# Pads and a new order of the SBUF pools in a two-layer decoder kernel: tiles that TensorE reads brought to multiples of 512 bytes

## The chip, the cores and the metric

The kernel runs on one core of a Trainium2 chip. The metric is device time in microseconds (us) of one launch, which holds the whole computation; weights are re-cut on the host before the launch and come from HBM. The kernel before was run three times: median 2026.53 us, from 2025.38 to 2033.36.

## The reference

Two decoder layers over x of 512 tokens x 1024 channels, in float32:

```python
for l in range(2):
    x = x + 0.5 * rmsnorm(swiglu_1(rmsnorm(x, g0)), g1)
    x = x +       rmsnorm(mixer_l(rmsnorm(x, g2)), g3)
    x = x + 0.5 * rmsnorm(swiglu_2(rmsnorm(x, g4)), g5)
# swiglu(h) = (silu(h @ wg) * (h @ wu)) @ wd, inner width 2816
# mixer_0: a gated depthwise causal convolution of 31 taps with LayerNorm and SiLU over 512 channels,
#          beside sliding-window attention (8 query heads, 2 key heads, ALiBi, sinks); both into one w_out
# mixer_1: "FoX", causal attention of 16 heads with forget gates, then w_out
```

## The kernel before, in words

**Products.** Every large float32 product is done in three passes of type float32r. An operand is split into `hi` and `lo` (`split`, L65: ScalarE makes `hi`, VectorE or GpSimd subtracts), and `mm3` (L69 to L74) adds hi.hi, hi.lo and lo.hi into one PSUM tile, on the lines 72, 73 and 74. Each pass is a load of 128 stationary columns and one product that streams the moving operand, mostly 512 columns of 4 bytes, 2048 bytes of each partition. In the profile's names `mm<-hhi,whi` the moving operand comes first, the stationary one second.

**Order of the work.** A SwiGLU half step (`ffn`, L188) works in eleven groups of two blocks of 128 inner columns. For each group, `gate_up` streams the normed tokens hT (`hhi`, `hlo`, channels on partitions, eight slices of 512 tokens) past four weight units of 1024 columns (`whi`, `wlo`), 24 products a unit, 96 a group; `evac` makes the activations `ahi`, `alo`. `down` of the group before streams the down weights (again `whi`, `wlo`) past `ahi`, `alo`: 48 products a group, four token blocks x two blocks x two halves x three passes. The first group and the last use products of 256 columns (`first_projs`, L102; `gate_up_half`, L260). The even mixer (`even`, L296) projects 14 units, runs the convolution's taps on VectorE, ScalarE and GpSimd while TensorE projects, then the attention, the LayerNorm and the output projection from `cT` (`chi`, `clo`). The odd mixer (`odd`, L552) projects 16 heads between the heads' scores and values. The queues' order is planned by the framework (line 887), which also sets the waits. All loads of weights go through the SP queue into the three `raw` buffers.

**Where tiles lie.** Pools are laid behind one another in each SBUF partition. Those on the left begin at byte 16512, in the order of their opening, and each tile is rounded up to 32 bytes; those on the right end at byte 229344. Within a pool the tiles follow in the order in which they are first asked for. Worked out by these sizes, the remainders of the start addresses modulo 512 are:

| tile | read by TensorE as | before | after the change |
|---|---|---|---|
| hT: `hhi`, `hlo` (pool `keep`) | moving in projections, stationary for the values of FoX | 224 | 0 |
| `whi`, `wlo` of the rings, and of `dring` on the left | stationary in projections, moving in down | 352 | 0 |
| `whi`, `wlo` of `dring` on the right (layer 1, second half step) | the same | 480 | 0 |
| `ahi`, `alo` | stationary in down | 352 | 0 |
| `chi`, `clo` | stationary in the output projection | 480 even, 352 odd | 0 |
| q, k, v of the even mixer | both | 480 | 0 |
| q, k, v tiles and `pT` of FoX | both | 352 | 0 |
| `yv` | moving, plain float32 | 352 | 0 |
| `wk` work tiles | stationary in transposes | 224 | 0 |
| `ident`, `ident16`, `tri` | transposes and masks | 128, 160, 416 | 288, 320, 64 |
| `alibi`, `ones` | masks, sums of the LayerNorm | 480, 160 | 64, 64 |

All slices that the products take step by multiples of 512 bytes, but for the first four FoX value weights, whose rows are 1088 bytes long (`VF = 256 + H`, L589).

**Names and lines that the steps touch.** `junk` (L132) is where ScalarE's squares for the norms go; nothing reads it. `ones` (L800) is read by the LayerNorm's sums (L480, L491, L502). `alibi` (L538) is built on GpSimd at the start of the even mixer and read by its scores (L414). `dring` (L193) is the down weights' pool. `rstd` (L122) is the norm's part on GpSimd.

Of the kernel before, what the change touches and what calls it, by code (L numbers as in the profile page):

```python
"""Two decoder layers (macaron SwiGLU, conv + sliding-window mixer, forgetting-attention mixer).

Every float32 product with large operands runs on the tensor engine in three float32r passes: an
operand is split exactly into hi (12 significant bits) and lo = x - hi (the other 12), and
a.b = hi.hi + hi.lo + lo.hi is accumulated in float32 PSUM.

Layouts: x is token-major, [128 tokens, 1024] for each of the four token blocks. A pre-norm's result
is transposed into channel-major hi/lo tiles [128, k, 512 tokens], which every projection reads.
"""
# [9 lines left out]
F32 = mybir.dt.float32  # L19
# [7 lines left out]
P = 128  # L27
S = 512
# [12 lines left out]
class Kernel:  # L41
    def __init__(self, ctx, tc, a):
        self.ctx, self.tc, self.nc, self.a = ctx, tc, tc.nc, a
        pool = lambda name, bufs, **kw: ctx.enter_context(tc.tile_pool(name=name, bufs=bufs, **kw))
        self.const = pool("const", 1)
        self.keep = pool("keep", 1)
        self.raws = pool("raws", 3)
        self.work = pool("work", 7)
        self.small = pool("small", 4)
        self.mm = pool("mm", 4, space=PSUM)  # L50
        self.acc = pool("acc", 4, space=PSUM)
# [17 lines left out]
    def mm3(self, out, a, b, start, stop):  # L69
        """out (+)= a.T @ b, each operand a (hi, lo) pair."""  # L70
        mm = self.nc.tensor.matmul
        mm(out, a[0], b[0], start=start, stop=False)  # L72
        mm(out, a[0], b[1], start=False, stop=False)  # L73
        mm(out, a[1], b[0], start=False, stop=stop)  # L74
# [6 lines left out]
    def unit(self, src, inner, pool=None, eng=None):  # L81
        """A [128, 1024] piece of a weight, loaded and split; its (hi, lo) as [128, 1024/inner, inner]."""
        pool = pool or self.ring
        raw = self.loaded.pop(0) if self.loaded else self.load(src)
        hi, lo = (pool.tile([P, 1024], F32R, name=n)[:, : raw.shape[-1]] for n in ("whi", "wlo"))
        with ExitStack() as after:
            for ins in self.guard:
                after.enter_context(self.tc.issue_after(ins.ins))
            self.split(hi, lo, raw, eng)
        return [z.rearrange("p (k c) -> p k c", c=inner) for z in (hi, lo)]  # L90

    def proj(self, out, u, toks=slice(0, S), m=P):
        """out[m, toks] = u.T @ h, u a unit of m columns."""
        for k in range(KD):
            self.mm3(out, [z[:, k, :m] for z in u], [z[:, k, toks] for z in self.hT], k == 0, k == KD - 1)
# [6 lines left out]
    def first_projs(self, srcs, pooled=3, pool=None):  # L102
        """Four units at once, the first half of the tokens ahead of the second."""
        units = [self.unit(s, P, pool, self.nc.gpsimd if n < pooled else None) for n, s in enumerate(srcs)]
        out = [self.psum() for _ in units]
        for half in range(2):
            toks = slice(half * 256, half * 256 + 256)
            for n, (o, u) in enumerate(zip(out, units)):
                self.proj(o[:, toks], u, toks)
                if self.begin:  # L110
                    self.begin.pop(0)()
                if n % 2:
                    self.turn()
        self.guard = self.turned
        return out
# [6 lines left out]
    def rstd(self, ss, eps):  # L122
        """(ss[0] + ss[1] + eps) ** -0.5 for a [128, 2] tile."""
        nc = self.nc
        ms = self.small.tile([P, 1], F32, name="ms")
        nc.gpsimd.tensor_scalar(ms, ss[:, 0:1], ss[:, 1:2], eps, ALU.add, ALU.add)
        r = self.small.tile([P, 1], F32, name="rstd")
        nc.gpsimd.tensor_tensor(r, ms, self.mhalf, ALU.pow)  # L128
        return r

    def square_sum(self, out, src, scale):
        junk = self.work.tile([P, 512], BF16, name="junk", bufs=1)  # L132
        self.nc.scalar.activation(junk, src, AF.Square, scale=scale, accum_out=out)  # L133

    def post(self, t, ys, gain, half_step):
        """x[t] += (0.5 or 1) * rmsnorm(y) * gain; ys are y's two halves, the later one last."""
# [13 lines left out]
    def pre(self, t, gain, order=(0, 1), helper=None):  # L150
        """h[t] = rmsnorm(x[t]) * gain, transposed and split into hT."""
# [18 lines left out]
    def turn(self, n=1):  # L170
        """Transposes and splits the pre-norm's oldest n token blocks that still wait for it."""
# [16 lines left out]
    def ffn(self, l, s, norms, nxt, held=None):  # L188
        nc, tc, a = self.nc, self.tc, self.a
        wg, wu, wd = (a[w][l, s] for w in ("ffn_w_gate", "ffn_w_up", "ffn_w_down"))  # L190
        with ExitStack() as ctx:
# [54 lines left out]
            gate_up(0)  # L246
            if held:
                held.close()
# [3 lines left out]
            # the last two groups of the down projection a token block at a time, the last group's gate  # L252
            # and up half the tokens at a time, so that the norms run under the other half's products
# [42 lines left out]
    def even(self, l, i, nxt):  # L296
# [3 lines left out]
        with ExitStack() as ctx:  # L300
# [6 lines left out]
            cw = late.tile([P, NC, CK], F32, name="cw")  # L307
            conv, att = ExitStack(), ExitStack()
# [4 lines left out]

            sink = pc.tile([P, 8], F32, name="sink")
# [5 lines left out]
            # per-channel parameters, channels on partitions  # L320
            cwr = self.wk()
            nc.sync.dma_start(cwr[:CK, :], a["conv_w"][i])
            for n, v in enumerate(("conv_b", "conv_ln_g", "conv_ln_b")):
                nc.sync.dma_start(vec[:, n, :], a[v][i].rearrange("(c p) -> p c", p=P),
# [12 lines left out]
            def glu(c, sg, pu):  # L337
                """u * sigmoid(gate), with the convolution's zeros ahead of it."""
# [10 lines left out]
            # the depthwise causal convolution: the later taps as products on ScalarE summed on GpSimd  # L349
# [19 lines left out]
            # q tile t holds heads t and t + 4, so that each lies on its kv head's partitions  # L369
            q = [pc.tile([P, NC, S], F32R, name=n) for n in ("qhi", "qlo")]  # L370
            k = [pc.tile([P, S], F32R, name=n) for n in ("khi", "klo")]
            v = [pc.tile([P, NT, P], F32R, name=n) for n in ("vhi", "vlo")]
# [25 lines left out]
            # sliding window attention; ALiBi and the window as one additive bias per head  # L398
# [70 lines left out]
            cT = [cat.tile([P, KD, S], F32R, name=n) for n in ("chi", "clo")]  # L469
            for c in range(NC):  # L470
# [6 lines left out]
            # LayerNorm over the conv channels (partitions): sums through the tensor engine  # L477
# [18 lines left out]
            # to all channels: ones.T @ diag(rstd)  # L496
# [11 lines left out]
            # the attention's half of the output projection  # L508
# [29 lines left out]
    def alibi(self, pool):  # L538
        """Per head, minus slope * distance inside the window and NEG outside it; exact in bfloat16."""
# [12 lines left out]
    def odd(self, l, i, nxt):  # L552
# [3 lines left out]
        with ExitStack() as ctx:  # L556
# [8 lines left out]
            # A head's scores in two products of 128 rows: qa.ka = qhi.khi - c (through a selector of the  # L565
            # head's rows of -c) and qc.kc = qhi.klo + qlo.khi
# [20 lines left out]
            # the values of four heads, [keys, head, (hi, lo), 64]; the first four's weights lie beside the gates'  # L587
# [19 lines left out]
            # c = cumsum(log sigmoid(zf + b_f)), heads on partitions;  # L607
            # log sigmoid(z) = min(z, 0) - log(1 + exp(-|z|))
            def gates():
# [10 lines left out]
                # minus c as hi (rows 64..) and lo (rows 96..)  # L620
# [32 lines left out]
            def transposed(pr):  # L653
                """Blocks of key tile kb, queries kb * 128 .. 512, as (hi, lo)."""
# [13 lines left out]
            def values(h, at):  # L668
# [6 lines left out]
                # rows 0..63 hold v's hi part, the others its lo part  # L675
# [12 lines left out]
            def early(t):  # L688
                """The first 12 heads' part of the output projection's later half."""
# [68 lines left out]
    def run(self):  # L758
        nc, a = self.nc, self.a
        self.x = [self.keep.tile([P, D], F32, name=f"x{t}") for t in range(NT)]  # L760
# [13 lines left out]
        # the clock of an idle tensor engine is halved: products that nothing reads, until x is there  # L774
# [23 lines left out]
    def constants(self):  # L798
        nc = self.nc
        self.ones = self.const.tile([P, P], F32, name="ones")  # L800
        nc.gpsimd.memset(self.ones, 1.0 / CC)
        self.ident16 = self.const.tile([P, P], BF16, name="ident16")
        nc.gpsimd.tensor_copy(self.ident16, self.ident)
        # 0 where key <= query, else NEG
# [3 lines left out]
        # pick[p, h] = 1 where p % 32 == h, for partitions 0..47 and 64..111  # L808
# [15 lines left out]
def _laid_out(i):  # L824
    """The arrays as the kernel reads them: each weight cut into [128, 1024] pieces, every piece contiguous."""
    import numpy as np

    def stationary(w):
        """[n, 1024, C] -> [n, C/128, 128 rows, 8 * 128]: column tile, row in its row tile, (row tile, column)."""
# [3 lines left out]
    def moving(w):  # L833
        """[n, 1024, 1024] -> [n, column half, row tile pair, 128 rows, 2 * 512]."""
# [9 lines left out]
    # conv gates and inputs by turns, k, v, then q heads t and t + 4 side by side  # L844
# [46 lines left out]
```

## Time and profile before

| what | value |
|---|---|
| median of three runs, lowest, highest | 2026.53, 2025.38, 2033.36 us |
| span of the profiled execution | 2025.8 us |
| the profiled execution's own time | not listed apart from the span; the span stands 0.7 us under the median |
| TensorE busy | 1951.0 us, 96% |
| VectorE, ScalarE, GpSimd busy | 986.5, 727.6, 285.5 us |
| mean granted TensorE clock | 0.974 |
| moved by DMA | 178.91 MB, 88 GB/s |

The span runs from the first to the last instruction on the core. [...]

### The profile page before, as it was taken

Reading aid. Unit: us, or ns where it says so; the run is one execution under the profiler, and the core shown is the slowest. Engines: PE = TensorE matmul, PEld = TensorE weight load, DVE = VectorE, ACT = ScalarE, POOL = GpSimd, SP = SyncE. Lnnn points to the kernel's source line nnn. Section 1 sums busy time; section 2 is a strip of 40 time slices with the busy share of each in tenths; the row PEclk is TensorE's granted clock in tenths of the full one; section 3 lists DMA queues with packets and bytes.
Section 4 is the critical chain, followed back from the end, with each engine's and each line's share of the span. In section 5 each row is a group of like instructions: output and inputs, shape, how many; then the busy total and the mean of one; then the engine's idle time right before and its main releaser. Section 6 shows DMA issues by size and latency. Waiting matters only on the chain.

```text
span 2025.8 us, 23961 instructions
## 1 busy us (share of the span) xinstructions
PE 1951.0 (96%) x9694; PEld 1630.3 (80%) x9694; DVE 986.5 (49%) x1351; ACT 727.6 (36%) x1230; POOL 285.5 (14%) x280
## 2 busy tenths in 40 slices
PE   8999999994899999999999999999999989999998
PEld 7888888883578888888988888898888888888887
DVE  6333333589866333333553333346666564333333
ACT  5322221363564322221342222226666543222221
POOL 2000000486512000000300000014222220000001
PEclk8999999997699999999999999999999999999999
DMA  6423232122022423232143232303112224232311
GB/s 213 130 83 104 83 104 73 44 63 73 21 74 93 136 84 103 91 99 76 54 160 104 83 104 87 100 23 113 54 42 65 95 81 139 91 103 84 104 53 42
DMA packets 51407, 178.91 MB, mean 88 GB/s; under 512 B 7361, under 2 KB 7361, under 8 KB 51296
## 3 DMA queue, kind: packets, MB, share of 16 engines
q1 hardware_dynamic: 51296, 177.38, 27.1%
q8 instruction: 76, 1.25, 0.3%
q14 instruction: 35, 0.29, 0.0%
HBM read 175.26 MB, written 2.10 MB: 88 GB/s over the span
## 4 chain that ended last, share of the span: by engine, by line
PE 84%; DVE 8%; ACT 3%; POOL 2%; issue 1%; DMA 1%; SPq 0%; POOLq 0%; DVEq 0%; ACTq 0%
PE mm L73 23%; PE mm L72 23%; PE mm L74 23%; PE acc L72 4%; PE acc L73 4%; PE acc L74 4%; DVE yv L356 4%; ACT junk L133 1%; DVE wlo L67 1%; PE mm L663 1%; PE mm L673 1%; PE acc L182 1%; POOL rstd L128 1%; DVE hlo L67 1%; DVE x L148 1%
## 5 line engine op out<-in xcount | busy, mean ns | idle before, releaser
L72 PE MATMUL mm<-hhi,whi 128*128 128x512 f32 (+1 forms) x1952 | 705.6, 364 | 13.6 <-DVE av L340 8.7
L73 PE MATMUL mm<-hlo,whi 128*128 128x512 f32 (+1 forms) x1952 | 707.2, 363 | 3.7 <-DVE hlo L67 3.5
L74 PE MATMUL mm<-hhi,wlo 128*128 128x512 f32 (+1 forms) x1952 | 706.9, 363 | 0.0
L67 ACT CAST whi<-raw 128x1024 fp32r<-128x1024 f32 x319 | 331.0, 1046 | 892.3 <-issue 261.1
L67 DVE TENSOR_TENSOR wlo<-raw,whi 128x1024 fp32r<-128x1024 f32 x287 | 351.6, 1238 | 387.4 <-ACT whi L67 378.2
L72 PEld LDWEIGHTS mm<-hhi,whi 128*128 128x128 f32 x1952 | 371.2, 191 | 75.7 <-DVE av L340 9.1
L73 PEld LDWEIGHTS mm<-hlo,whi 128*128 128x128 f32 x1952 | 372.0, 191 | 65.0 <-DVE hlo L67 5.1
L74 PEld LDWEIGHTS mm<-hhi,wlo 128*128 128x128 f32 x1952 | 372.1, 191 | 60.2
L144 POOL TENSOR_TENSOR wk<-ysb,gpost 128x512 f32<-128x512 f32 x16 | 21.1, 1321 | 1395.4 <-issue 1024.3
L206 DVE TENSOR_TENSOR wk<-mm,wk 128x512 f32<-128x512 f32 (+1 forms) x96 | 62.1, 647 | 302.9 <-PE mm L74 260.7
L243 DVE TENSOR_TENSOR ysb<-mm,ysb 128x512 f32<-128x512 f32 x128 | 88.6, 692 | 163.9 <-PE mm L74 163.9
L72 PE MATMUL acc<-whi,ahi 128*128 128x512 f32 x352 | 137.6, 391 | 0.0
L74 PE MATMUL mm<-whi,alo 128*128 128x512 f32 x352 | 137.6, 391 | 0.0
L74 PE MATMUL acc<-whi,alo 128*128 128x512 f32 x352 | 137.6, 391 | 0.0
L73 PE MATMUL acc<-wlo,ahi 128*128 128x512 f32 x352 | 137.5, 391 | 0.0
L73 PE MATMUL mm<-wlo,ahi 128*128 128x512 f32 x352 | 137.5, 391 | 0.0
L72 PE MATMUL mm<-whi,ahi 128*128 128x512 f32 x352 | 137.3, 392 | 0.0
L67 POOL TENSOR_TENSOR wlo<-raw,whi 128x1024 fp32r<-128x1024 f32 x32 | 78.7, 2474 | 80.5 <-ACT whi L67 72.9
L366 POOL TENSOR_TENSOR yg<-yg,pr 128x512 f32<-128x512 f32 x52 | 84.5, 1632 | 29.6 <-ACT pr L364 13.7
L356 DVE SCALAR_TENSOR_TENSOR yv<-av,cw,yv 128x512 f32<-128x512 f32 x64 | 87.3, 1412 | 0.1
L205 ACT ACTIVATE wk<-mm 128x512 f32<-128x512 f32 (+1 forms) x96 | 53.4, 557 | 68.3 <-PE mm L74 68.3
L74 PEld LDWEIGHTS acc<-whi,alo 128*128 128x128 f32 x352 | 66.2, 188 | 14.6
(190 smaller groups left out, 2054.0 us busy)
## 6 DMA issues: line engine op xcount, KB each, us to landing
raw<-in_ffn_w_gate_dram SPq DMA_DIRECT2D x88, 512.0 KB, 3.5
raw<-in_ffn_w_up_dram SPq DMA_DIRECT2D x88, 512.0 KB, 4.1
raw<-in_ffn_w_down_dram SPq DMA_DIRECT2D x88, 512.0 KB, 3.5
raw<-in_fox_w_qk_dram SPq DMA_DIRECT2D x16, 512.0 KB, 3.6
raw<-in_ab_w_in_dram SPq DMA_DIRECT2D x14, 512.0 KB, 3.4
raw<-in_ab_w_out_dram SPq DMA_DIRECT2D x8, 512.0 KB, 3.4
raw<-in_fox_w_out_dram SPq DMA_DIRECT2D x8, 512.0 KB, 3.5
gpre<-in_norm_g_dram SPq DMA_DIRECT2D x6, 512.0 KB, 5.1
```

The source lines that it names most:

```text
L67: return nc.scalar.copy(hi, src), (eng or nc.vector).tensor_tensor(lo, src, hi.bitcast(F32), ALU.subtract)
L72: mm(out, a[0], b[0], start=start, stop=False)
L73: mm(out, a[0], b[1], start=False, stop=False)
L74: mm(out, a[1], b[0], start=False, stop=stop)
L128: nc.gpsimd.tensor_tensor(r, ms, self.mhalf, ALU.pow)
L133: self.nc.scalar.activation(junk, src, AF.Square, scale=scale, accum_out=out)
L144: (nc.vector if n else nc.gpsimd).tensor_tensor(yg[n], y, gain[:, h * 512 : h * 512 + 512], ALU.mult)
L205: nc.scalar.activation(sg, pg, AF.Silu)
L206: nc.vector.tensor_tensor(av, pu, sg, ALU.mult)
L243: nc.vector.tensor_tensor(ysb[t], p, ysb[t], ALU.add)
L356: r = nc.vector.scalar_tensor_tensor(yv[c], av[c][:, k : k + S], cw[:, c, k : k + 1], yv[c], ALU.mult, ALU.add)
L366: nc.gpsimd.tensor_tensor(yg, yg, pr, ALU.add)
```

## The change

The tiles move; no arithmetic changes. In `const` a pad of 160 bytes and the tile `junk` come in, `ones` goes out; the pool `small` is opened right behind it, so that `keep` and all that follows on the left begin at byte 19968, which is 39 x 512. On the right, pads of 480 bytes in `dring` (layer 1, second half step) and in `cat` (even mixer), and of 416 bytes in the even mixer's pool, make up for the 480 in 229344. `junk` is one tile kept for the whole run where it was asked for anew each time out of one buffer. `ones` is made at the start of the even mixer, in the pool `late`. The even mixer's q, k and v are asked for ahead of `sink`, `nsink` and `alibi`, which so lie at the pool's end. A loop variable is renamed, and comments are blanked so that line numbers stay close.

```diff
         self.const = pool("const", 1)
+        self.small = pool("small", 4)
+
+        self.const.tile([P, 40], F32, name="pad")
         self.keep = pool("keep", 1)
         self.raws = pool("raws", 3)
         self.work = pool("work", 7)
-        self.small = pool("small", 4)
...
     def square_sum(self, out, src, scale):
-        junk = self.work.tile([P, 512], BF16, name="junk", bufs=1)
+        junk = self.junk
...
             gate_up(0)
+            if l % 2 and s:
+                dring.tile([P, 120], F32, name="pad", bufs=1)
             if held:
...
             cw = late.tile([P, NC, CK], F32, name="cw")
+            self.ones = late.tile([P, P], F32, name="ones")
+            nc.gpsimd.memset(self.ones, 1.0 / CC)
             conv, att = ExitStack(), ExitStack()
...
+            q = [pc.tile([P, NC, S], F32R, name=n) for n in ("qhi", "qlo")]
+            k = [pc.tile([P, S], F32R, name=n) for n in ("khi", "klo")]
+            v = [pc.tile([P, NT, P], F32R, name=n) for n in ("vhi", "vlo")]
             sink = pc.tile([P, 8], F32, name="sink")
...
-            q = [pc.tile([P, NC, S], F32R, name=n) for n in ("qhi", "qlo")]
-            k = [pc.tile([P, S], F32R, name=n) for n in ("khi", "klo")]
-            v = [pc.tile([P, NT, P], F32R, name=n) for n in ("vhi", "vlo")]
+
+            pc.tile([P, 104], F32, name="pad")
...
             cT = [cat.tile([P, KD, S], F32R, name=n) for n in ("chi", "clo")]
+            cat.tile([P, 120], F32, name="pad")
...
         nc, a = self.nc, self.a
+        self.junk = self.const.tile([P, 512], BF16, name="junk")
         self.x = [self.keep.tile([P, D], F32, name=f"x{t}") for t in range(NT)]
...
     def constants(self):
         nc = self.nc
-        self.ones = self.const.tile([P, P], F32, name="ones")
-        nc.gpsimd.memset(self.ones, 1.0 / CC)
```

## Rows read from the trace of the kernel before

**Rows 1.** The page, busy us and the span in 40 slices (tenths).

```profile
PE 1951.0 (96%) x9694; PEld 1630.3 (80%) x9694; DVE 986.5 (49%) x1351; ACT 727.6 (36%) x1230; POOL 285.5 (14%) x280
...
PEclk8999999997699999999999999999999999999999
```

**Rows 2.** The page, the chain that ended last, by engine and by line.

```profile
PE 84%; DVE 8%; ACT 3%; POOL 2%; issue 1%; DMA 1%; SPq 0%; POOLq 0%; DVEq 0%; ACTq 0%
PE mm L73 23%; PE mm L72 23%; PE mm L74 23%; PE acc L72 4%; PE acc L73 4%; PE acc L74 4%; DVE yv L356 4%; ACT junk L133 1%; DVE wlo L67 1%; PE mm L663 1%; PE mm L673 1%; PE acc L182 1%; POOL rstd L128 1%; DVE hlo L67 1%; DVE x L148 1%
```

**Rows 3.** TensorE's groups by shape: count | busy us, mean ns | idle before.

```profile
L72 PE MATMUL mm<-hhi,whi 128*128 128x512 f32 x1344 | 533.6, 397 | 11.0 <-DVE av L340 8.7 <-DVE klo L67 2.3
...
L72 PE MATMUL mm<-hhi,whi 128*128 128x256 f32 x608 | 172.0, 290 | 2.6 <-ACT hhi L67 2.6
...
L72 PE MATMUL mm<-whi,hhi 128*128 128x256 f32 x96 | 28.0, 292 | 0.0
...
L480 PE MATMUL acc<-yv,ones 128*128 128x512 f32 x8 | 3.6, 592 | 0.0
```

**Rows 4.** TensorE's timeline, half step 1: start us, duration us, instruction.

```profile
135.07 0.39 PE L74 MATMUL acc<-whi,alo 128*128 128x512 f32 x1
...
145.97 0.40 PE L72 MATMUL mm<-hhi,whi 128*128 128x512 f32 x1
...
168.36 0.39 PE L74 MATMUL acc<-whi,alo 128*128 128x512 f32 x1
```

**Rows 5.** TensorE's timeline, half step 4: gate and up, then down.

```profile
1740.14 0.40 PE L72 MATMUL mm<-hhi,whi 128*128 128x512 f32 x1
...
1762.44 0.40 PE L74 MATMUL acc<-whi,alo 128*128 128x512 f32 x1
...
1762.92 0.40 PE L73 MATMUL acc<-wlo,ahi 128*128 128x512 f32 x1
...
1773.60 0.39 PE L72 MATMUL mm<-hhi,whi 128*128 128x512 f32 x1
```

**Rows 6.** TensorE's timeline, 256 columns: end of half step 1, and FoX values.

```profile
345.69 0.28 PE L72 MATMUL mm<-hhi,whi 128*128 128x256 f32 x1
...
357.21 0.39 PE L72 MATMUL mm<-whi,ahi 128*128 128x512 f32 x1
...
1428.40 0.28 PE L673 MATMUL mm<-pThi,vv 128*128 128x256 f32 x1
...
1428.63 0.22 PE L673 MATMUL mm<-pThi,vv 128*128 128x128 f32 x1
```

**Rows 7.** Stretches: length; busy us (count) of PE, PEld, DVE, ACT, POOL; clock; DMA.

```profile
135.00:146.00 11.00, 11.00 (x51) 9.07 (x50) 5.56 (x8) 2.65 (x3) 0.00 (x0) 1.00 0.13 48
...
409.00:412.00 3.00, 3.00 (x15) 3.00 (x15) 1.67 (x2) 0.58 (x1) 2.70 (x5) 0.50 0.02 4
...
455.00:530.00 75.00, 38.71 (x144) 28.22 (x142) 74.16 (x74) 27.07 (x51) 48.69 (x27) 0.72 0.18 60
...
1762.40:1773.60 11.20, 11.20 (x49) 9.05 (x49) 5.56 (x8) 2.65 (x3) 0.00 (x0) 1.00 0.14 47
```

**Rows 8.** TensorE's timeline at the lower clock, and the plain float32 sums.

```profile
410.57 0.41 PE L74 MATMUL mm<-hhi,wlo 128*128 128x256 f32 x1
...
411.64 0.41 PE L73 MATMUL mm<-hlo,whi 128*128 128x256 f32 x1
...
562.67 3.59 PE L480 MATMUL acc<-yv,ones 128*128 128x512 f32 x8
```

**Rows 9.** The page: the cast of a weight unit, and the convolution's taps.

```profile
L67 ACT CAST whi<-raw 128x1024 fp32r<-128x1024 f32 x319 | 331.0, 1046 | 892.3 <-issue 261.1
...
L356 DVE SCALAR_TENSOR_TENSOR yv<-av,cw,yv 128x512 f32<-128x512 f32 x64 | 87.3, 1412 | 0.1
```

**Rows 10.** GpSimd's last norm before the even mixer, and TensorE's reads of `alibi`.

```profile
401.90 0.56 POOL L128 TENSOR_TENSOR rstd<-ms,mhalf 128x1 f32<-128x1 f32 x1
...
L414 PE MATMUL acc<-alibi,ident x32: 229/286/396, 487.5 to 560.7; 128*128 128x256 bf16 x24, 128*128 128x128 bf16 x8
```

More of the change, by code (lines that the diff above doesn't have):

```diff
@@ L322, in even @@
             nc.sync.dma_start(cwr[:CK, :], a["conv_w"][i])
-            for n, v in enumerate(("conv_b", "conv_ln_g", "conv_ln_b")):
-                nc.sync.dma_start(vec[:, n, :], a[v][i].rearrange("(c p) -> p c", p=P),
+            for n, name in enumerate(("conv_b", "conv_ln_g", "conv_ln_b")):
+                nc.sync.dma_start(vec[:, n, :], a[name][i].rearrange("(c p) -> p c", p=P),
                                   allow_slow_non_contiguous=True)
```

## The prediction

> **What bounds the kernel now.** Read first the busy shares and the clock's slices: TensorE is busy 1951.0 us, 96% of the span, at the full granted clock in nearly every slice; VectorE is busy 49% [rows 1]. The chain that ended last agrees: 84% of it is TensorE's, almost all on the three lines of `mm3`, 8% VectorE's [rows 2]. So what counts is how long one product holds TensorE. The mean durations by shape don't tell it, because neighbouring products overlap: 397 ns for 512 columns [rows 3] is a latency. The reader takes the distance from one start to the next out of the timeline, and divides over a whole stretch in which TensorE waits for nothing.
>
> Four such distances carry this prediction; the offsets are those of the kernel section, modulo 512.
> - Down projection, half steps 1 to 3 (moving 352, stationary 352): 48 products from 135.07 to 145.97 us, 227.1 ns each [rows 4].
> - Gate and up, same half step (moving 224, stationary 352): 96 products to 168.36 us, 233.2 ns [rows 4].
> - Down projection of half step 4, whose weights lie in the pool on the right (moving 480, stationary 352): 48 products from 1762.44 to 1773.60 us, 232.5 ns; gate and up beside it, from 1740.14, 232.3 ns [rows 5].
> - 256 columns (224 against 352): 96 products from 345.69 to 357.21 us, 120.0 ns [rows 6].
>
> The second and third are the point. The two downs issue the same instructions on the same shapes at the same clock, with the same work on the other engines (VectorE 5.56 us in both windows, ScalarE 2.65) [rows 7]; the fourth costs 5.4 ns a product more. Where the tiles lie is the difference. In the fast down both operands begin at one remainder of 512, in the slow ones at two different ones. The FoX values again have both at 352: two products of 256 columns take 0.23 us there [rows 6], 115 ns each, against 120.0.
>
> How far could it fall? [...] No float32r operand here begins at 0, so the trace doesn't show that place itself.
>
> **The change, part by part.** The pads, the order of the pools and `junk`'s move put hT, the rings, the products' operands, cT and q, k, v all at 0, so every pair has equal remainders. [...] I take 227.1: it is the row nearest in kind, the same instruction with equal remainders. For 256 columns I take the same share, 0.974, 3.1 ns a product (the row for equal remainders gives 5, read to 10 ns).
>
> The sum, with counts by shape [rows 3]. Gate, up and the mixers' projections are 1344 products of 512 columns on each of three lines, 4032: 864 in each half step (nine groups of 96), 336 in FoX (14 heads of 24), 240 in the even mixer.
> - Half steps 1 to 3: 2592 x 6.1 ns = 15.8 us.
> - Half step 4: 864 x 5.2 = 4.5 us, and its downs, 432 + 96 = 528 products x 5.4 = 2.9 us.
> - The other 1584 downs stay at 227.1: 0.
> - FoX projections: 336 x 6.1 = 2.0 us.
> - 256 columns: (608 + 96) x 3 = 2112; without 192 at the even mixer's start, 1920 x 3.1 = 6.0 us.
> - The even mixer's output projection (chi at 480), 192 x 5.4 = 1.0 us.
> - The even mixer's 240: from 455 to 530 us VectorE is busy 74.16 of 75 us and TensorE 38.71 [rows 7], on the convolution's taps (87.3 us) [rows 9]. What TensorE saves there it waits out: 0.
>
> That is 32.2 us; I take 1 off for the heads, which also wait for ScalarE and VectorE. Against the profiled execution's span of 2025.8 us it leaves 1994.6; around that span stands 0.7 us to the median of the runs, 2026.53, so 1995.3.
>
> What covers the work behind the products: a weight unit feeds 24 of them, 5.6 us now and 5.45 then, and its cast takes ScalarE 1.05 us [rows 9]; in the down's window VectorE is busy half of the time, the DMA engines 0.13 of it [rows 7]. Nothing there becomes late at 3% more. If that cover went, the cast's 1.05 us a unit would show.
>
> The rest is edits at nothing. `junk` is written by ScalarE alone, in order, before and after: no wait goes or comes. `ones` is now set by one instruction of GpSimd when the even mixer begins, on bytes where the down projection's weights lay, so it waits for the last product that reads those. Queued behind it on GpSimd is the mask `alibi`. But GpSimd's norms of that half step need the same products anyhow, and the last `rstd` ahead of the mask is at 401.90 us; the mask is first read at 487.5 [rows 10], 85 us later, and `ones` at 562.67 [rows 8]. That is its cover; without it the instruction's own time would count, well under a us for 128 columns. No DMA is added; the sinks' load goes to other bytes on the same queue, behind `conv_w`, so SP's order has no reason to change. Should the plan come out in another order in that mixer, I bound it by the 8.7 us for which the projections wait for the gated values there [rows 3], either way.
>
> `ident`, `ident16`, `tri`, `alibi` and `ones` don't come to 0 (288, 320, 64, 64, 64 by my sizes). [...]
>
> [...] The trace: equal downs at 227.1 and 232.5 ns [rows 4, 5]. [...]
>
> **The rivals.**
> [...]
> 2. *The place isn't what the rows differ by*, or the order of the plan eats it. Then about 2026. Gate/up and down differ in kind anyway; against it stand the two downs, alike but for the pool.
> 3. *Slower: equal starts collide.* If both of TensorE's reads now start on the same line and meet in each product at 240 ns, the 512 columns lose 2592 x 6.8 + 864 x 7.7 + 336 x 6.8 + 1584 x 12.9 + 528 x 7.5 ns = 51 us, and 256 columns at the same ratio 1920 x 3.5 ns = 7: 2085. It decides as soon as the downs of half steps 1 to 3, where the forecast is no change, rise past about 235 ns while gate and up stay. Against: equal remainders are the fastest rows there are.
>
> **How the numbers follow.** Forecast 0.45, its own range 1985 to 2005 (the 256-column term from 3 to 5 ns, a few us of re-planning). Rival 1: 0.25, spread from 1893 to 1985. Rival 2: 0.15. Rival 3: 0.15, from just above the runs to 2085. Three runs of one kernel lie 8 us apart, so 0.5%, some 10 us, is about what a measurement can tell from no change. Faster 0.70, same 0.15, slower 0.15. The range 1900 to 2035 leaves out the tip of rival 1 and most of rival 3.
>
> **What would show it.** In the changed profile: gate and up at 227 ns (96 products in 21.8 us), half step 4's down at 227, the other downs unchanged, 256 columns near 117. Downs falling below 227 is rival 1; gate and up still at 233 is rival 2; downs above 230 is rival 3. In the even mixer the VectorE-bound stretch should keep its length. I'm wrong if TensorE's distances improve and the time doesn't: then a weight's cast or its DMA is late.

## The result, and the profile after

The changed kernel takes 1996.7 us, median of four runs from 1996.38 to 1999.3; the kernel before, run once more beside it, 2027.1 us, median of four from 2025.38 to 2033.36. The ratio is 0.9856, 95% interval 0.984 to 0.9872: 30.4 us less. The profiled execution has a span of 1994.6 us, 31.2 less than before's 2025.8, and a time of its own of 1996.38.

The page of the changed kernel: busy us and the clock's slices, and the chain that ended last by engine, answer to [rows 1, 2].

```profile
PE 1920.4 (96%) x9694; PEld 1626.4 (82%) x9694; DVE 985.4 (49%) x1351; ACT 726.3 (36%) x1230; POOL 284.9 (14%) x280
...
PEclk8999999996699999999999999999999999999999
...
PE 85%; DVE 8%; ACT 3%; POOL 2%; issue 1%; DMA 1%; SPq 0%; DVEq 0%; POOLq 0%; ACTq 0%
```

The same instructions on every engine, and still TensorE's time: its busy time fell by 30.6 us, that of the others by about 1. The groups by shape say little, as before: 392 ns against 397 [rows 3] is a latency, though the fall of 5 ns hints at the place.

```profile
L74 PE MATMUL mm<-hhi,whi 128*128 128x512 f32 x1344 | 526.8, 392 | 10.7 <-DVE av L349 9.6 <-DVE klo L69 1.1
...
L74 PE MATMUL mm<-hhi,whi 128*128 128x256 f32 x608 | 171.2, 289 | 2.7 <-ACT hhi L69 2.7
```

The distances come from TensorE's timeline of the changed kernel (start us, duration us, instruction; line numbers here are two above before's):

```profile
43.19 0.40 PE L74 MATMUL mm<-hhi,whi 128*128 128x512 f32 x1
...
131.39 0.39 PE L76 MATMUL acc<-whi,alo 128*128 128x512 f32 x1
...
142.27 0.39 PE L74 MATMUL mm<-hhi,whi 128*128 128x512 f32 x1
...
164.03 0.39 PE L76 MATMUL acc<-whi,alo 128*128 128x512 f32 x1
...
338.11 0.28 PE L74 MATMUL mm<-hhi,whi 128*128 128x256 f32 x1
...
349.63 0.40 PE L74 MATMUL mm<-whi,ahi 128*128 128x512 f32 x1
...
646.70 0.40 PE L74 MATMUL mm<-hhi,whi 128*128 128x512 f32 x1
...
1308.24 0.28 PE L74 MATMUL mm<-hhi,whi 128*128 128x256 f32 x1
...
1648.63 0.40 PE L74 MATMUL mm<-hhi,whi 128*128 128x512 f32 x1
...
1747.71 0.39 PE L74 MATMUL mm<-hhi,whi 128*128 128x512 f32 x1
...
1769.47 0.39 PE L76 MATMUL acc<-whi,alo 128*128 128x512 f32 x1
...
1780.35 0.39 PE L74 MATMUL mm<-hhi,whi 128*128 128x512 f32 x1
...
1943.55 0.28 PE L74 MATMUL mm<-hhi,whi 128*128 128x256 f32 x1
```

Half step 1: down 131.39 to 142.27, 48 products, 226.7 ns each (before 227.1 [rows 4]); gate and up to 164.03, 96 products, 226.7 ns (before 233.2). Half step 4: gate and up 1747.71 to 1769.47, 226.7 ns, down to 1780.35, 226.7 ns (before 232.3 and 232.5 [rows 5]). One value everywhere. The 256 columns: 338.11 to 349.63, 96 products, 120.0 ns, to the hundredth of a us what before took [rows 6].

Where the 31.2 us came from needs a few more starts of before:

```profile
45.04 0.39 PE L72 MATMUL mm<-hhi,whi 128*128 128x512 f32 x1
...
656.74 0.40 PE L72 MATMUL mm<-hhi,whi 128*128 128x512 f32 x1
...
1329.71 0.28 PE L72 MATMUL mm<-hhi,whi 128*128 128x256 f32 x1
...
1672.06 0.39 PE L72 MATMUL mm<-hhi,whi 128*128 128x512 f32 x1
...
1974.38 0.28 PE L72 MATMUL mm<-hhi,whi 128*128 128x256 f32 x1
```

| stretch, from one of these starts to the next | before, us | after, us | less by |
|---|---|---|---|
| to the first product of 512 columns | 45.04 | 43.19 | 1.85 |
| half step 1, to its first 256-column product at the end (345.69 [rows 6]) | 300.65 | 294.92 | 5.73 |
| its end and the even mixer | 311.05 | 308.59 | 2.46 |
| half steps 2 and 3 and what lies between | 672.97 | 661.54 | 11.43 |
| end of half step 3, and FoX | 342.35 | 340.39 | 1.96 |
| half step 4 | 302.32 | 294.92 | 7.40 |
| the end | 51.42 | 51.05 | 0.37 |

So 24.6 us lie in the rows of the four half steps, where TensorE streams almost without a pause: it is busy in all 300.65 and 302.32 us of half steps 1 and 4 before, and in 672.14 of the 672.97 of half steps 2 and 3. The first line isn't the change's: two more profiled executions of the changed kernel reach that product at 44.19 and 44.25 us, one of a kernel with unequal starts (the second experiment) at 43.88. The row of FoX varies too: the same two executions of the changed kernel take 340.43 and 341.77 us for it.

The even mixer. The first and the last of the 64 taps on VectorE (columns: duration min/median/max, first and last start), before:

```profile
L356 DVE SCALAR_TENSOR_TENSOR yv<-av,cw,yv x64: 735/1745/2902, 419.2 to 527.7; 128x512 f32<-128x512 f32 x64
```

after:

```profile
L365 DVE SCALAR_TENSOR_TENSOR yv<-av,cw,yv x64: 735/1746/2896, 409.8 to 518.2; 128x512 f32<-128x512 f32 x64
```

108.5 us and 108.4: the stretch that VectorE bounds gave nothing. What the mixer did give lies ahead of it. Windows of before (busy us and counts of PE, PEld, DVE, ACT, POOL; granted clock; DMA):

```profile
403.00:407.00 4.00, 2.22 (x17) 2.21 (x18) 1.66 (x4) 1.13 (x2) 3.50 (x9) 0.87 0.03 10
407.00:411.00 4.00, 3.32 (x16) 2.92 (x15) 3.39 (x5) 2.12 (x3) 3.51 (x7) 0.50 0.00 0
```

The clock fell there to 0.50, from a stretch in which TensorE was busy 2.22 of 4 us on; in the changed kernel the same work, again with one stretch of 2.22 us in 4, kept 1.00:

```profile
395.00:399.00 4.00, 2.22 (x22) 2.01 (x21) 1.81 (x4) 0.91 (x2) 3.44 (x10) 1.00 0.03 12
399.00:403.00 4.00, 2.85 (x22) 2.42 (x21) 3.37 (x5) 2.09 (x4) 3.54 (x7) 1.00 0.00 0
```

It isn't a fixed gift: in a later profile of the changed kernel (the one beside experiment 6) the clock stood at 0.65 from 399 to 403 us. The way from the first 256-column product at the end of half step 1 to the mixer's first product of 512 columns took 75.5 us there, against 74.3 here and 76.3 before.

### The profile page after: what moved, and what is told of

Read it like the earlier page. It is cut to its first block, busy times and chain, and to the rows that moved or that the text cites. A ratio compares the mean times of both kernels' runs of the same rounds, so it can differ in the third digit from the quotient of the medians.

```text
span 1994.6 us, 23959 instructions
## 1 busy us (share of the span) xinstructions
PE 1920.4 (96%) x9694; PEld 1626.4 (82%) x9694; DVE 985.4 (49%) x1351; ACT 726.3 (36%) x1230; POOL 284.9 (14%) x280
## 4 chain that ended last, share of the span: by engine, by line
PE 85%; DVE 8%; ACT 3%; POOL 2%; issue 1%; DMA 1%; SPq 0%; DVEq 0%; POOLq 0%; ACTq 0%
PE mm L75 23%; PE mm L76 23%; PE mm L74 23%; PE acc L74 4%; PE acc L75 4%; PE acc L76 4%; DVE yv L365 4%; ACT junk L135 1%; DVE wlo L69 1%; PE mm L671 1%; PE mm L681 1%; DVE hlo L69 1%; DVE x L150 1%; POOL rstd L130 1%; POOL ms L128 0%
## 5 line engine op out<-in xcount | busy, mean ns | idle before, releaser
L74 PE MATMUL mm<-hhi,whi 128*128 128x512 f32 (+1 forms) x1952 | 698.0, 360 | 13.5 <-DVE av L349 9.6
L75 PE MATMUL mm<-hlo,whi 128*128 128x512 f32 (+1 forms) x1952 | 699.7, 359 | 4.7 <-DVE hlo L69 4.5
L76 PE MATMUL mm<-hhi,wlo 128*128 128x512 f32 (+1 forms) x1952 | 698.7, 359 | 0.0
```

## The experiments

Three theories. **Pair**: what counts is that the moving and the stationary operand of a product start at equal remainders. **Zero**: what counts is that they start at multiples of 512. **Side moves**: the gain comes from `junk`, `ones`, the pools' order or the new plan. All diffs are against the changed kernel.

**1. Every pair equal, at 224 instead of 0.** Only the pads' sizes differ.

```diff
-        self.const.tile([P, 40], F32, name="pad")
+        self.const.tile([P, 96], F32, name="pad")
...
-                dring.tile([P, 120], F32, name="pad", bufs=1)
+                dring.tile([P, 64], F32, name="pad", bufs=1)
...
-            pc.tile([P, 104], F32, name="pad")
+            pc.tile([P, 48], F32, name="pad")
...
-            cat.tile([P, 120], F32, name="pad")
+            cat.tile([P, 64], F32, name="pad")
```

> The changed kernel with its pads made larger or smaller so that every tile that it brought to 0 modulo 512 lies at 224 instead, left and right alike; nothing else differs from it. Theory PAIR (what counts is that the moving operand and the stationary one begin at the same remainder of 512; the remainder itself hardly does): gate, up and down all at 226.7 to 227.2 ns a product, in half step 4 as well, and 1995 to 2000 us. Theory ZERO (what counts is that tiles begin on a multiple of 512): gate, up and down at 232 ns or more, at or above the 2027 us of the kernel before.

Measured: 1998.08 us against 2027.0 of before, ratio 0.9858 (0.9842 to 0.9875). TensorE's timeline of this kernel, half step 1:

```profile
143.12 0.39 PE L74 MATMUL mm<-hhi,whi 128*128 128x512 f32 x1
...
164.88 0.39 PE L76 MATMUL acc<-whi,alo 128*128 128x512 f32 x1
...
175.76 0.39 PE L74 MATMUL mm<-hhi,whi 128*128 128x512 f32 x1
```

Gate and up 21.76 us for 96, down 10.88 for 48: 226.7 ns both, as in the changed kernel. Zero falls: a multiple of 512 is worth nothing beyond the equality.

**2. The side moves alone.** `junk`, `ones`, `small`, q, k and v stay where the change puts them; other pads bring the remainders back to 224, 352 and 480.

```diff
-        self.const.tile([P, 40], F32, name="pad")
+        self.padded = False
+        self.const.tile([P, 96], F32, name="pad")
...
-        return self.work.tile([P, 512], F32, name="wk")
+        t = self.work.tile([P, 512], F32, name="wk")
+        if not self.padded:
+            self.padded = True
+            self.work.tile([P, 32], F32, name="pad", bufs=1)
+        return t
...
-            if l % 2 and s:
-                dring.tile([P, 120], F32, name="pad", bufs=1)
...
-            pc.tile([P, 104], F32, name="pad")
...
-            cat.tile([P, 120], F32, name="pad")
```

> The changed kernel's other edits alone (junk, ones, small, q k v ahead of the sinks), with pads that put hT, rings, down weights and products back to the remainders of the kernel before (224, 352, 480). PAIR and ZERO both: 233.2, 227.1 and 232.5 ns a product as before, and 2022 to 2028 us, since the moves themselves are worth 0 to 4 us. Rival SIDE (the gain came from the moved tiles and the new plan): the products still at 233 but the time under 2010 us.

Measured: 2025.7 us, ratio 1.0 (0.9989 to 1.0011). Its timeline, half steps 1 and 4:

```profile
133.98 0.39 PE L81 MATMUL acc<-whi,alo 128*128 128x512 f32 x1
...
144.88 0.40 PE L79 MATMUL mm<-hhi,whi 128*128 128x512 f32 x1
...
167.27 0.39 PE L81 MATMUL acc<-whi,alo 128*128 128x512 f32 x1
...
1762.34 0.40 PE L81 MATMUL acc<-whi,alo 128*128 128x512 f32 x1
...
1773.54 0.40 PE L79 MATMUL mm<-hhi,whi 128*128 128x512 f32 x1
```

Down 227.1 and gate and up 233.2 ns in half step 1, as before; down 233.3 in half step 4, where before had 232.5. The picture is that of before. The side moves are worth nothing that can be measured, and Pair carries all of it.

**3. How equal is equal?** Three maps move the weights (and, for the downs, the activations with them or against them) by another amount in each half step. In the first two, a table gives the offsets in bytes of the ring, of the down weights and of the activations for the four half steps:

```diff
+OFF = {(0, 0): (32, 32, 32), (0, 1): (64, 64, 64), (1, 0): (128, 128, 128), (1, 1): (256, 256, 256)}
...
+            ra, dm, st = OFF[l, s]
+            right = l % 2 and s
+            for p, n in ((self.ring, ra), (dring, 0 if right else (dm - ra) % 512), (act, (st - (ra if right else dm)) % 512)):
+                if n:
+                    p.tile([P, n // 4], F32, name="off", bufs=1)
...
-                dring.tile([P, 120], F32, name="pad", bufs=1)
+                dring.tile([P, (480 - OFF[l, s][1]) % 512 // 4], F32, name="pad", bufs=1)
```

> The changed kernel with the rings, down weights and products of half steps 1 to 4 moved by 32, 64, 128 and 256 bytes; hT stays at 0. So gate and up have pairs (moving, stationary) of (0, 32), (0, 64), (0, 128), (0, 256), and the downs (32, 32), (64, 64), (128, 128), (256, 256). PAIR: all four downs at 226.7 to 227.2 ns; gate and up slower in each, 233 ns at 128 and 228 to 234 at the other differences. ZERO: the four downs at 230 ns or more; gate and up between, since their moving operand is still at 0. About 2015 to 2025 us by PAIR.

Measured: 2019.44 us. The miss is 256 bytes: its half step 4 runs like the changed kernel, as the timeline shows (96 products in 21.76 us, 48 in 10.88).

```profile
1738.10 0.39 PE L77 MATMUL mm<-hhi,whi 128*128 128x512 f32 x1
...
1759.86 0.39 PE L79 MATMUL acc<-whi,alo 128*128 128x512 f32 x1
...
1770.74 0.39 PE L77 MATMUL mm<-hhi,whi 128*128 128x512 f32 x1
```

The second map has the same code with these offsets:

```diff
+OFF = {(0, 0): (96, 0, 320), (0, 1): (192, 448, 0), (1, 0): (384, 0, 160), (1, 1): (480, 32, 0)}
```

> The changed kernel with other offsets by half step: gate and up (0, 96), (0, 192), (0, 384), (0, 480) and the downs (0, 320), (448, 0), (0, 160), (32, 0), as (moving, stationary) modulo 512. PAIR: every one of the eight slower than 227.2 ns, none faster than 226.7; a pair with the same difference costs the same whichever operand is off (448 against 0 as 0 against 64 of the other map). ZERO: the pairs with the moving operand at 0 all cost alike.

Measured: 2034.51 us, slower than before, since here no pair is equal, the downs included.

The third gives the unit's view inside a wider tile an offset of its own (in floats: for 512 columns, for 256), so that steps below 32 bytes can be tried:

```diff
+OFF = {(0, 0): (4, 8), (0, 1): (2, 16), (1, 0): (60, 40), (1, 1): (52, 56)}
...
-        hi, lo = (pool.tile([P, 1024], F32R, name=n)[:, : raw.shape[-1]] for n in ("whi", "wlo"))
+        w = 1152 if pool in self.wide else 1024
+        hi, lo = (pool.tile([P, w], F32R, name=n)[:, off : off + raw.shape[-1]] for n in ("whi", "wlo"))
```

> The changed kernel with the weight units of 512-column products 16, 8, 240 and 208 bytes off in half steps 1 to 4, and those of 256-column products 32, 64, 160 and 224 bytes off. The map so far: 226.7 ns at a difference of 0 or 256, 229.0 at 192, 233 to 234 at all others of multiples of 32. PAIR says that 16 and 8 are slower than 227 too; if reads are matched by lines of 16 bytes or more, 8 stays at 226.7. At 256 columns the unequal pairs took 117.3 to 118.5 ns and the equal one 120.0, so all four are expected under 119.

Measured: 2019.7 us. Its timeline, gate and up in half step 1 (16 bytes apart) and in half step 2 (8 bytes apart):

```profile
142.52 0.39 PE L77 MATMUL mm<-hhi,whi 128*128 128x512 f32 x1
...
164.28 0.39 PE L79 MATMUL acc<-whi,alo 128*128 128x512 f32 x1
...
690.35 0.40 PE L77 MATMUL mm<-hhi,whi 128*128 128x512 f32 x1
...
712.49 0.40 PE L78 MATMUL acc<-wlo,ahi 128*128 128x512 f32 x1
```

226.7 and 230.6 ns (230.7 from the unrounded starts). The expectation missed here: 16 bytes cost nothing, where Pair said slower, and 8 bytes do. At 256 columns 160 bytes took 119.9 ns, not under 119.

The three maps with the kernel before and the runs above, each from stretches of the timeline without waits, ns a product. The distance is the stationary start less the moving one, modulo 512; a value with a number in brackets was measured at that distance, the same one the other way round:

| distance, bytes | 512 columns, gate and up | 512 columns, down | 256 columns |
|---|---|---|---|
| 0 | 226.7 | 226.7 to 227.5 | 119.9 |
| 8 | 230.7 | | |
| 16 | 226.7 | | |
| 32 | 233.4, 233.3 (480) | 233.4 (480) | 118.3, 116.7 to 117.8 (480) |
| 64 | 233.3 | 233.4 | 113.3 to 117.8, 117.8 (448) |
| 96 | 234.3 | | 117.3 to 118.7 |
| 128 | 232.3 to 233.3, 232.4 to 233.3 (384) | 232.4 to 233.3 (384) | 118.6 to 120.0, 118.6 to 120.0 (384) |
| 160 | | 233.3 | 119.9 |
| 192 | 229.0, in one group of nine 233.3 | 233.2 (320) | 117.8 |
| 208 | 231.9 | | |
| 224 | | | 116.7 |
| 240 | 226.7 | | |
| 256 | 226.7 | | 119.9 |

At 512 columns distances of 0, 16, 240 and 256 took 226.7 ns in gate and up, the 8 bytes in between 230.7. So by these runs what must agree, to 16 bytes, is the remainder modulo 256, not 512. With 256 columns the order is turned round: the equal pairs, at 119.9 ns, are among the slowest there, and no distance took more than 120.0 ns.

A distance doesn't always give one value. In the kernel before, gate and up of half step 1 begin at 224 and 352 in every group, and yet the first group (45.04 above to 67.33) takes 232.2 ns a product (232.3 from the unrounded starts) and the later ones 233.2. The products wander about their mean: from 228 to 241 ns in the first group, mostly 229 and 238 by turns in the later ones, while the equal pairs of the changed kernel take 226 or 227 each. With 256 columns the first group of half step 2 (648.20 to 656.74 above) takes 118.6 ns where the last groups take 120.0:

```profile
67.33 0.40 PE L72 MATMUL acc<-whi,ahi 128*128 128x512 f32 x1
...
648.20 0.28 PE L72 MATMUL mm<-hhi,whi 128*128 128x256 f32 x1
```

The fastest 256 columns seen are in the first group of half step 2 of the first map, 64 bytes apart: 72 products at 113.3 ns, against 117.8 at the same distance in that half step's last groups (the third map shows the same two values):

```profile
646.29 0.28 PE L77 MATMUL mm<-hhi,whi 128*128 128x256 f32 x1
...
654.45 0.39 PE L77 MATMUL mm<-hhi,whi 128*128 128x512 f32 x1
```

What sets the two apart wasn't tried.

**4. Which of the two neighbours pays?** `wlo` alone lies 128 bytes off, `whi` stays at 0. In the three passes (hhi past whi, hlo past whi, hhi past wlo) `wlo` is loaded for one of them, while the one ahead of it still streams: in the changed kernel the load for the third pass at 150.21 us runs from 149.98 to 150.17, under the second pass, which begins at 149.98 and lasts 0.39 us.

```diff
-        hi, lo = (pool.tile([P, 1024], F32R, name=n)[:, : raw.shape[-1]] for n in ("whi", "wlo"))
+        hi = pool.tile([P, 1024], F32R, name="whi")[:, : raw.shape[-1]]
+        if pool is self.split_pool:
+            self.split_pool = None
+            pool.tile([P, 32], F32, name="off", bufs=1)
+        lo = pool.tile([P, 1024], F32R, name="wlo")[:, : raw.shape[-1]]
...
+            if not (l % 2 and s):
+                dring.tile([P, 96], F32, name="off", bufs=1)
+            else:
+                act.tile([P, 96], F32, name="off", bufs=1)
```

> The changed kernel with wlo, and wlo alone, 128 bytes off in the half steps' rings: hhi, hlo and whi stay at 0. Of three products in a row the weights change from whi (hi.hi, hi.lo) to wlo (lo.hi). PAIR, with the load of the next weights as the partner: the product under which wlo is loaded (hlo against whi) is the slow one, about 233 to 240 ns to the next start, the others 226.7. PAIR, with the product's own weights as the partner: the third (hhi against wlo) is the slow one. By both about 229 ns in the mean of gate and up. If neither, all three take 226.7.

Measured: 2011.5 us. In gate and up of the half steps the first pass, whose own and next weights are equal with it, takes 226.7 ns; the second, during which the weights 128 off are loaded, 232.5; the third, which uses them while the next, equal ones are loaded, 234.2 (means over the stretches, unrounded starts). The timeline's sum agrees: 96 products in 22.19 us are 231.1 each.

```profile
176.91 0.39 PE L74 MATMUL mm<-hhi,whi 128*128 128x512 f32 x1
...
199.10 0.39 PE L76 MATMUL acc<-whi,alo 128*128 128x512 f32 x1
```

Two of the three pay, where each theory had one and 229 ns in the mean. They cost 5.8 + 7.5 ns a three, with 1152 threes in the four half steps 15.3 us; the run stands 12 to 15 us over the changed kernel's three medians. A meeting of the load's reads with the stream's, which is the author's guess and seen in no run, would account for the second pass, but not for the third by itself. Either a product is also held up when it streams past unequal weights that were loaded before, or a delay lasts beyond the load that caused it. The kernel before has slow products that fit a lasting delay: the first three products of its equal down, right behind unequal gate and up, fill 0.70 us from 135.07 [rows 4], some 232 ns each, though they and the loads beside them are equal; the other 45, to 145.97, take 226.7.

```profile
135.77 0.39 PE L74 MATMUL acc<-whi,alo 128*128 128x512 f32 x1
```

No run here separates the two.

**5. Is the load what is left?** In the changed kernel 512 columns take 226.7 ns and 256 take 120.0. The 256 columns more cost 106.7 ns; an estimate from these two is 213.3 for 512 columns (the 512 / 2.4 below) and 13.3 ns that don't grow with the columns. If these 13.3 were the load of the next weights, half as many columns would cost less. Gate and up of half step 2 load 64 columns in six of eight slices; the other 64 columns of these are left out of the sums.

```diff
+    def proj_64(self, src):
+        out = self.psum()
+        u = self.unit(src, P)
+        for k in range(KD):
+            m = P if k in (0, KD - 1) else 64
+            self.mm3(out[:m], [z[:, k, :m] for z in u], [z[:, k, :] for z in self.hT], k == 0, k == KD - 1)
+        return out
...
-                    evac(f, self.proj_new(wg[f]), self.proj_new(wu[f]))
+                    new = self.proj_64 if l == 0 and s else self.proj_new
+                    evac(f, new(wg[f]), new(wu[f]))
```

> The changed kernel, in which half step 2's gate and up use 64 stationary columns in place of 128 for the row tiles 1 to 6 (columns 64 to 127 of these are left out of the sums). Theory LOAD (the 13.3 ns over 512 / 2.4 that every product still loses come from reading the 128 columns of the next weights beside it): 220 ns a product, half of the loss. Theory FIXED (each product loses them whatever is loaded): 226.7 ns.

Measured: 2000.12 us, and the products there take 229.2 ns, not less than 226.7 but more, which neither theory said. A smaller load doesn't help; where the constant 13.3 ns come from stays open.

**6. Both at once: equal for 512 columns, 224 bytes apart for 256.** The table's last column offers 3.3 ns at 224 bytes for some 1920 products (64 bytes, with its 113.3 in first groups, wasn't tried for this). The units of 1152 floats of the third map are used, with offsets 0 and 56 floats in all half steps; beside it the changed kernel itself.

```diff
+OFF = {(0, 0): (0, 56), (0, 1): (0, 56), (1, 0): (0, 56), (1, 1): (0, 56)}
```

> The changed kernel with the weight units of the half steps' 256-column products (first group, last group: 1536 products) 224 bytes off hT, all 512-column products left at equal remainders. From the maps: 116.7 ns in place of 120.0 at 256 columns, 226.7 kept at 512. That is 1536 x 3.3 ns, at most 5 us; the first groups also wait for the norms, so 3 to 5 us under the changed kernel beside it. If the two lengths don't want different places after all, the same time as the changed kernel.

> The changed kernel itself, on the same chip as the version with mixed offsets: 1995 to 1999 us, 226.7 and 120.0 ns.

Measured: 2012.73 us, ratio 0.9928 (0.9914 to 0.9942), against 1997.87 and 0.9862 (0.9844 to 0.9879) for the changed kernel on the same chip. The products do what the map says, 116.7 and 226.7 ns, and yet it is 15 us slower than the changed kernel, where 3 to 5 less were expected. The waits between 600 and 670 us, TensorE's (us in total, times, longest), of the mixed kernel:

```profile
PE acc L188 <- DVE wk L173: 13.5, 3, 6.5
```

and of the changed kernel beside it:

```profile
PE acc L184 <- DVE wk L169: 0.9, 1, 0.9
```

TensorE's transposes of the normed tokens wait for VectorE, 13.5 us against 0.9. ScalarE's casts of the next weights come later; that these hold VectorE up is the author's reading, not tried. ScalarE's timeline of the mixed kernel (in brackets the idle time before, and for what):

```profile
595.68 1.05 ACT L72 CAST whi<-raw 128x1024 fp32r<-128x1024 f32 x1 [10.25 <-PE mm L79]
628.41 2.92 ACT L72 CAST whi<-raw 128x1024 fp32r<-128x1024 f32 x3
```

In the changed kernel five casts run from 585.67 to 598.10 us, here one. By the addresses, the wider units reach bytes of the even mixer's tiles that were clear of them; that this overlap is what delays the casts is argued, not tried.

**7. The same with less room.** Units of 1088 floats, in half steps 1 and 3 only, where no wider ring stands behind the even mixer. Such a unit is 4352 bytes long, so every other tile begins 256 bytes further on: the 512-column pairs are 0 or 256 apart, those of 256 columns 224 or 480.

```diff
-        hi, lo = (pool.tile([P, 1024], F32R, name=n)[:, : raw.shape[-1]] for n in ("whi", "wlo"))
+        w = 1088 if pool in self.wide else 1024
+        hi, lo = (pool.tile([P, w], F32R, name=n)[:, off : off + raw.shape[-1]] for n in ("whi", "wlo"))
...
+            o5, o2 = OFF[l, s]
+            self.wide = [] if s else [self.ring]
+            o2 = 0 if s else o2
```

> As the changed kernel, but the ring tiles of half steps 1 and 3 are 1088 floats wide a unit instead of 1024, and the 256-column products there read weights that start 224 bytes (modulo 512) away from their hT. Theory 'a 256-column product is 3.3 ns shorter with unequal starts': 116.7 ns in half steps 1 and 3 (768 products), 120 in 2 and 4, 226.7 for all 512-column products; 768 x 3.3 = 2.5 us less than the changed kernel beside it, 1994 to 1996 us. Rival 'any wider ring moves the weight casts of the next step behind something': TensorE gaps of several us at the transposes before half steps 2 or 4 and 1999 us or more. No difference (within 1 us) if the 2.5 us come back as a wait at the end of the two half steps.

> The changed kernel itself, on the chip of the run above, as the measure for it: 1997 to 1998 us, 226.7 ns a 512-column product, 120 ns a 256-column product.

Measured: 2005.08 us, ratio 0.9889 (0.9874 to 0.9904), against 1999.37 and 0.986 (0.9843 to 0.9876). The products do as wanted again (116.7 and 226.7 ns), and the rival holds, though at another place than it named: the mixed kernel is 1.9 us ahead when half step 2's 512-column products begin, 3.1 behind when half step 3's do and 4.1 behind at half step 4's. The three casts for half step 3 that begin at 977.39 us in the changed kernel begin at 985.85 there. Nothing tried here beats the changed kernel.

## Why the prediction came out

The forecast was 1995 us, 30 to 31 below; the median came to 1996.7, within the forecast's own range of 1985 to 2005. The mechanism is the one named, and experiments 1 and 2 show it from both sides. The sum, though, is right partly because its errors cancel.

- **Equal remainders set the distance**: held. The result itself excludes rival 1 (a place at 0 is far faster than equal starts elsewhere): at 0 the products take 226.7 ns, and in experiment 1 they take the same at 224. Its 1893 us counts with 214 ns for 512 columns and 107 for 256 at the full granted clock, which no run shows; equal pairs took 226.7 and 120.0. Experiment 2 excludes rival 2 (the place isn't it), and the downs, which end at 226.7, rival 3, whose 240 ns are the mean from 1762.44 to 1762.92 us before [rows 5].
- **Half steps 1 to 3, gate and up, 15.8 us**: a little too small. They fell from 233.25 to 226.67 ns, 6.58 a product, but in the first group of 512 columns of each half step only from 232.3 to 226.9, 5.4: 2304 x 6.58 + 288 x 5.4 = 16.7. The prediction's own rows had 233.2 and 232.3 at the same two starts and took the one for half steps 1 to 3, the other for half step 4; the remainders alone don't fix the value to a ns.
- **Half step 4, 4.5 + 2.9 us**: about right. 864 x 5.7 = 4.9, and the downs 528 x 5.7 = 3.0.
- **The other downs, 0**: 0.3 ns each in the mean, 1584 x 0.3 = 0.5 us. It is the first three products of each stretch, which no longer take 232 ns (experiment 4).
- **FoX, 2.0 us**: 1.96 in the table, though only 0.6 in one of the two later profiles of the changed kernel.
- **256 columns, 6.0 us**: the step that failed. At the ends of the half steps they stay at 120.0 ns; in the first groups of half steps 1 to 3 they were at 118.7 and now take 120.0 too. The step carried the share 0.974 over from 512 columns, and leaned on two FoX starts read to 10 ns, in a place that also differs in the operands; unrounded, those two distances are 116 and 119 ns. Experiment 3's table shows that at 256 columns equality is no gain at all (119.9 ns), and 32 to 96 bytes apart (113.3 to 118.7) or 224 (116.7) would be. The sum leaves out the 192 at the even mixer's start; no run shows whether the place counts at a granted clock of 0.50, where five of them stood 214 ns apart before [rows 7, 8].
- **The even mixer**: 0 in VectorE's stretch, as said (108.5 and 108.4 us). The 2.5 us of its row in the table, where 1.0 was forecast, are 2.0 ahead of the mixer's 512-column products, where the clock's fall counts in, 0.7 from its output projection, and small differences.
- **`ones`, `junk`, the pools' order, 0**: held, by experiment 2's ratio of 1.0.
- **The 1 us taken off** for the heads didn't show in this profile; FoX gave its whole term.
- **The 0.7 us from span to run**: too small. Each run of these kernels stands some 1.8 us above its span, as 1996.38 above 1994.6. The forecast span, 1994.6, is the measured one to 0.1 us, and that is luck, as the sum below shows.

The 6.0 us too much at 256 columns were made up by 1.3 of gate and up (0.9 in half steps 1 to 3 and 0.4 in half step 4), 0.6 of the downs, 1.5 in the even mixer's row, 1 that was taken off in vain and, in the profiled span, 1.85 at the start that other executions don't repeat; the 0.2 over are small losses in other rows. Against the medians the gain is 30.4 us.

## What to carry to other kernels

Where TensorE streams float32r back to back, take the distance between starts (226.7 and 233.2 ns here), not the mean duration (392 and 397), and compare it over places that differ only in where the tiles lie: 6.6 ns of 233 were lost to two starts that differ modulo 256, and 4.4 of 231 where only `wlo`, the weights of every third product, was off. For streams of 512 columns make the remainders of moving and stationary tiles equal; which remainder it was, 0 or 224, didn't matter here (226.7 ns at both), and pads of 160 to 480 bytes did it. For 256 columns this gained nothing (120.0 ns at the ends of the half steps, before and after). A share found at one width is not to be carried to another: 0.974 at 512 columns was 1.0 there. And a wider tile may cost more than the better place gives: with units of 1152 floats the casts came later and the time was 15 us longer (2012.73 against 1997.87), where 3 to 5 us less were expected.

## What the runs showed of the hardware that was not expected

- The time of an equal pair isn't in proportion to its columns: 226.7 ns at 512 and 120.0 at 256, which leaves, by an estimate from these two, 13.3 ns a product that don't grow with them. With a load of 64 columns instead of 128 the product took longer (229.2 ns), not less.
- 256 bytes apart took the 226.7 ns of 0 at 512 columns, and so did 16 bytes to either side (16 and 240); 8 bytes took 230.7.
- At 256 columns no unequal distance took more than 120.0 ns, which is what the equal one takes, and most took less: 116.7 at 224 bytes, and at 64 bytes 113.3 in one place and 117.8 in another.
- Unequal pairs didn't keep one pace: in the kernel before, at the same two starts, 512 columns took 232.3 or 233.2 ns in the mean, single products of the first group 228 to 241, and three equal products behind them still took some 232.
- Weights off by 128 bytes slowed both the product during whose stream they were loaded (232.5 ns) and the one that used them (234.2 ns), against 226.7 for the first pass.
